# FFN-out's second Strassen half with accumulating loads on POOL, a shifted finish, and RG-LRU's input products placed later

## The chip, the cores and the metric

The kernel runs on one core of one Trainium2 chip. The metric is the device time of one execution in microseconds; the median of several executions counts. One more execution, made with the hardware profiler, gives the profile and the trace from which the rows below are.

## The reference

A hybrid encoder layer on 1024 + 512 positions of width 1024, float32. The parts that the change touches:

```python
xc = _centred_dwconv(xr, conv_w, conv_b)
rec = _rglru(xc, ..., False) + _rglru(xc, ..., True)
...
r = sigmoid(einsum(xb, wa) + ba)
i = sigmoid(einsum(xb, wx) + bx)
log_a = -RG_C * r * softplus(-lam)
a = exp(log_a)
u = sqrt(-expm1(2.0 * log_a)) * (i * xf)
_, h = associative_scan(comb, (a, u), reverse=reverse, axis=1)
...
fg, fu = split(h2 @ w_ffn_in, 2, axis=-1)
ff = (silu(fg) * fu) @ w_ffn_out
x = x + gt2[:, None] * ff
...
return _rmsnorm(x, final_g)
```

The hidden width of the FFN is 2816, in 22 column blocks of 128. Branch A (convolution, two RG-LRUs) stands early in the program, then come attention, the merge, FFN-in and, at the end, FFN-out.

## The kernel before

Every float32 product is three matmuls on high and low parts (hi·hi, hi·lo, lo·hi). The high part is a cast on ACT, the low part a subtraction on DVE, so each operand passes ACT and then DVE. Engines run their own instructions in the order of the program text; the text weaves helpers between matmuls by hand (`slots`, `bbuild`, `aprep`, the table `late`).

**RG-LRU** works on eight column blocks j of 128 channels, each a tile of 128 x 1536. While PE computes block j's input and its gate column, ACT and DVE finish the block before it. For each direction dd (0, 1) `decay(dd)` does on DVE L550 and L551 (from ACT's exponential and tanh) and L552, the input product i·xc; `roots(dd)` does on ACT L558 and L559 (square root; needs a table load); `scan(dd)` does on DVE L565 and the scans L570. `csplit` makes the high and low part xs of the next block (ACT L518, DVE L519), `gw_split` those of its gate weights (ACT L499, DVE L500). `gate(cc, dd)` multiplies xs by ghi and glo on PE (L532 to L534) into a bank of PSUM, and ACT empties it through a sigmoid into r and i (L535). `second` spreads these over six slots. Eleven buffers are passed around, so that the new i can take the place of one that the scan of the block before still reads.

**FFN-out** is one level of Strassen: seven products (PRODO, in the order 3, 1, 5, 2, 4, 6, 7), each of eleven K blocks and six pairs of row tiles. A step is one product for one pair: 33 matmuls, and there are 42 steps (n). The B operand of a product is a half of `w_ffn_out` or the sum or difference of two: products 3 and 4 subtract, 1, 6 and 7 add, 5 and 2 take one half alone. `bload` brings the two halves of a weight (256 KB each) by SP into one of two buffers, `bbuild` combines them (DVE L1274), casts (ACT L1275) and subtracts (DVE L1278). The A operands come by POOL (`aload`, L1306, 704 KB), are combined if need be (L1322), cast (L1323) and split (L1326). `take` adds a finished product to the accumulators `acc` (12 row tiles of 1024, in halves F1 and F2).

**The seam.** FFN-in's last products (PE L1446 to L1448 on tiles top, slot, woh, wol; emptied by ACT L1464 to L1478 and DVE L1468 to L1496; its weights combined at L1375 and split at L1359; results stored by SP, L1451, to ffd and ffx) run while `bbuild` makes the first eleven weights.

**The finish.** When the last product has been added to a half of `acc`, `squares` multiplies it by gt2 (DVE L1554), adds x1 (L1555; loaded by SP), and ACT squares and sums it (L1557). `norm1` and `norm2` make the row factors, `fin` scales both halves (DVE L1581) and stores them from POOL. The table `late` says at which step and K block. The last step's 512 columns are done in two parts of 256 (L1714 to L1717 for each) and closed by the last norm and two stores.

## Time and profile before

| | us |
|---|---|
| median of 3 executions | 2866.76 (2866.01 to 2868.51) |
| profiled execution | 2862.92 |
| its span | 2861.0 |
| PE busy | 2787.7 (97%) |
| DVE busy | 1925.6 (67%) |
| ACT busy | 1212.4 (42%) |
| POOL busy | 266.0 (9%) |

The span runs from the first to the last instruction of the profiled execution; 1.9 us of its time lie outside. Busy shares are means over all stages. A timeline row tells when an instruction started, how long it took and what its engine waited for ahead of it; a row of PE's waits tells what it waited for, us in total, how often, and the longest. A window row has the stretch, its length, busy time (and instructions) of PE, PE's weight loads, DVE, ACT and POOL, then the granted clock as a share of full speed, the DMA engines' share, and GB/s.

### The profile page before, as it was taken

How to read it: one execution, taken by the hardware profiler on the slowest of the kernel's cores; microseconds unless marked ns; L12 is line 12 of the kernel's file. 1: busy time of each engine (PE TensorE's matmuls, PEld its weight loads, DVE VectorE, ACT ScalarE, POOL GpSimd, SP SyncE). 2: the span in 40 equal slices, each digit the busy share in tenths (PEclk: the TensorE clock that was granted, in tenths of full speed). 3: DMA queues.
4: the chain of work that ended last, by engine and by line, in shares of the span. 5: the costliest groups of instructions: out<-in, count | busy, mean ns of one | idle time of the engine just before them, and what ended most of it. 6: DMA issues, size and time to landing. Idle time of an engine off the chain costs nothing. (4 is left out here: it accounts for less than half of the span.)

```text
span 2861.0 us, 38290 instructions
## 1 busy us (share of the span) xinstructions
PE 2787.7 (97%) x14165; PEld 2340.4 (82%) x14165; DVE 1925.6 (67%) x3615; ACT 1212.4 (42%) x2384; POOL 266.0 (9%) x365
## 2 busy tenths in 40 slices
PE   8999999999999999999999999999999999999997
PEld 4877777877777777777778877799999999977886
DVE  7487777555555555554367856599889888766787
ACT  6375766333333333224432015454444444344443
POOL 0000000000000000000153331101000000001002
PEclk9999999999999999999999999999999999999998
DMA  6211011201011011111367764567544444386685
GB/s 238 69 36 67 34 54 48 77 30 34 34 34 35 34 37 37 40 34 52 108 215 272 243 201 127 177 195 209 163 132 156 137 117 123 121 275 245 224 268 186
DMA packets 184395, 351.55 MB, mean 123 GB/s; under 512 B 20264, under 2 KB 99496, under 8 KB 183952
## 3 DMA queue, kind: packets, MB, share of 16 engines
q1 hardware_dynamic: 160016, 254.21, 28.0%
q0 software_dynamic: 24048, 94.63, 9.6%
q8 instruction: 111, 1.82, 0.3%
q14 instruction: 76, 0.62, 0.1%
q10 hardware_dynamic: 144, 0.26, 0.0%
HBM read 264.19 MB, written 84.85 MB: 122 GB/s over the span
## 5 line engine op out<-in xcount | busy, mean ns | idle before, releaser
L159 PE MATMUL mm<-hh,whi 128*128 128x512 f32 x1632 | 662.4, 406 | 2.8 <-DVE hh L292 2.3
L161 PE MATMUL mm<-hh,wlo 128*128 128x512 f32 x1632 | 641.3, 393 | 0.0
L160 PE MATMUL mm<-hl,whi 128*128 128x512 f32 x1632 | 639.7, 392 | 1.0 <-DVE hl L293 0.8
L159 PEld LDWEIGHTS mm<-hh,whi 128*128 128x128 f32 x1632 | 311.2, 191 | 71.3 <-issue 7.2
L161 PEld LDWEIGHTS mm<-hh,wlo 128*128 128x128 f32 x1632 | 307.5, 188 | 68.3
L160 PEld LDWEIGHTS mm<-hl,whi 128*128 128x128 f32 x1632 | 309.0, 189 | 63.5 <-DVE hl L293 4.4
L150 DVE TENSOR_TENSOR wlo<-wraw,whi 128x1024 fp32r<-128x1024 f32 x94 | 115.5, 1235 | 196.2 <-ACT whi L149 196.1
L747 ACT ACTIVATE sm<-sm,sg 128x192 f32<-128x192 f32 (+2 forms) x288 | 114.3, 397 | 303.4 <-DVE sg L742 303.0
L149 ACT CAST whi<-wraw 128x1024 fp32r<-128x1024 f32 x96 | 96.3, 1005 | 197.7 <-PE mm L160 124.4
L1375 DVE TENSOR_TENSOR sum<-wf 128x512 f32<-128x512 f32 x220 | 155.4, 707 | 1.5
L1377 ACT CAST woh<-sum 128x512 fp32r<-128x512 f32 x148 | 92.0, 622 | 151.4 <-DVE sum L1375 146.5
L742 DVE CUSTOM_DVE_ANT_0 sm<-sd,mk 128x192 f32<-128x192 f32 (+2 forms) x288 | 72.9, 291 | 117.0 <-PE sd L735 64.3
L668 DVE SCALAR_TENSOR_TENSOR t<-mm,rp 128x512 f32<-128x512 f32 x72 | 49.8, 692 | 150.2 <-PE mm L161 150.2
L1446 PE MATMUL mm<-top,woh 128*128 128x384 f32 x348 | 116.7, 335 | 3.3 <-DVE flat L1479 3.2
L1448 PE MATMUL mm<-top,woh 128*128 128x384 f32 x348 | 116.3, 334 | 0.0
L1447 PE MATMUL mm<-top,woh 128*128 128x384 f32 x348 | 116.2, 334 | 0.0
L1359 DVE TENSOR_TENSOR woh<-sum,woh 128x512 fp32r<-128x512 f32 x148 | 101.1, 683 | 0.6 <-ACT woh L1377 0.5
L857 DVE CUSTOM_DVE_ANT_0 jk<-ada 128x1024 bf16<-128x1024 f32 x64 | 80.5, 1271 | 23.6 <-DMA ada<-in_w_ada_dram 16.1
L1448 PE MATMUL sd<-top,woh 128*128 128x384 f32 x240 | 80.2, 334 | 0.0
L1446 PE MATMUL sd<-top,woh 128*128 128x384 f32 x240 | 80.2, 334 | 0.0
L1447 PE MATMUL sd<-top,woh 128*128 128x384 f32 x240 | 80.2, 334 | 0.0
L161 PE MATMUL mm<-rh,wlo 128*128 128x512 f32 x192 | 75.2, 392 | 3.8 <-DVE wlo L150 3.8
(452 smaller groups left out, 6386.6 us busy)
## 6 DMA issues: line engine op xcount, KB each, us to landing
wf<-in_w_fi_dram SPq DMA_DIRECT2D x88, 512.0 KB, 4.0
wraw<-in_w_in_dram SPq DMA_DIRECT2D x68, 512.0 KB, 3.5
wo<-in_w_fo_dram SPq DMA_DIRECT2D x132, 256.0 KB, 4.2
ffd<-flat SPq DMA_DIRECT2D x88, 192.0 KB, 4.0
ada<-in_w_ada_dram SPq DMA_DIRECT2D x32, 512.0 KB, 4.3
ffx<-flat SPq DMA_DIRECT2D x66, 192.0 KB, 2.3
wol<-ffd POOLq DMA_DIRECT2D x18, 704.0 KB, 4.9
gated<-gs POOLq DMA_DIRECT2D x48, 256.0 KB, 3.1
```

The costliest lines, as they stand in the source:

```text
L149: s.copy(out=hi, in_=t)
L150: eng.tensor_tensor(out=lo, in0=t, in1=hi.bitcast(F32), op=ALU.subtract)
L159: pe.matmul(ps, lhsT=hi(k), rhs=xh(k), start=a, stop=False)
L160: pe.matmul(ps, lhsT=hi(k), rhs=xl(k), start=False, stop=False)
L161: pe.matmul(ps, lhsT=lo(k), rhs=xh(k), start=False, stop=z)
L747: s.activation(out=sm[:, c], in_=sm[:, c], func=AF.Exp, scale=-1.0, bias=sg[:, u, x:x + 1], accum_out=sg[:, u, x + 1:x + 2])
L1359: v.tensor_tensor(out=r[:, CH:], in0=t, in1=f32(r[:, :CH]), op=ALU.subtract)
L1375: v.tensor_tensor(out=t, in0=wraws[p, a], in1=wraws[p, b], op=op)
L1377: s.copy(out=r[:, :CH], in_=t)
L1446: pe.matmul(ps, lhsT=hi, rhs=bh[:, k], start=k == 0 and not more, stop=False, skip_group_check=more)
L1447: pe.matmul(ps, lhsT=hi, rhs=bl[:, k], start=False, stop=False, skip_group_check=more)
L1448: pe.matmul(ps, lhsT=lo, rhs=bh[:, k], start=False, stop=k == 3, skip_group_check=more)
```

## The change

**RG-LRU.** `decay` loses the input product; it becomes `inputs(dd)`, and `second` has the two decays in slots one and two, ahead of `csplit` and `gw_split`, and the two input products in slot four.

On DVE, from a block's last convolution to its second scan, before (a, r and i are the two directions' tiles, xs and glo the next block's operands):

```order
 L550 SCALAR_TENSOR_TENSOR a_1427<-a_1427,r_1275 128x1536
 L551 SCALAR_TENSOR_TENSOR r_1275<-a_1427 128x1536
 L552 TENSOR_TENSOR i_1276<-i_1276,xc 128x1536
 L519 TENSOR_TENSOR xs_1459<-xc,xs_1458 128x1536
 L500 TENSOR_TENSOR glo_762<-graw,ghi_761 64x4x64 x2
 L550 SCALAR_TENSOR_TENSOR a_1430<-a_1430,r_1349 128x1536
 L551 SCALAR_TENSOR_TENSOR r_1349<-a_1430 128x1536
 L552 TENSOR_TENSOR i_1350<-i_1350,xc 128x1536
 L565 TENSOR_TENSOR i_1276<-i_1276,r_1275 128x1536
```

and now:

```order
 L550 SCALAR_TENSOR_TENSOR a_1427<-a_1427,r_1275 128x1536
 L551 SCALAR_TENSOR_TENSOR r_1275<-a_1427 128x1536
 L550 SCALAR_TENSOR_TENSOR a_1430<-a_1430,r_1349 128x1536
 L551 SCALAR_TENSOR_TENSOR r_1349<-a_1430 128x1536
 L519 TENSOR_TENSOR xs_1473<-xc,xs_1472 128x1536
 L500 TENSOR_TENSOR glo_762<-graw,ghi_761 64x4x64 x2
 L557 TENSOR_TENSOR i_1276<-i_1276,xc 128x1536
 L557 TENSOR_TENSOR i_1350<-i_1350,xc 128x1536
 L570 TENSOR_TENSOR i_1276<-i_1276,r_1275 128x1536
```

The second L551 moved ahead of three others, L519 and L500 moved back by one instruction's time, and the first product with r (L565, now L570) stands where it stood.

**The weights of FFN-out.** Their loads go from SP to POOL, the A operands' from POOL to SP. For the products that add, the second half is loaded with an accumulating transfer on top of the first (`accum_op`), so the DVE addition goes and a weight needs half a buffer: four weights are in flight instead of two. A base load is issued when the low part of the weight that held its place is done, the accumulating load one weight later. The first load stands one column earlier, low parts are put off to the next column or slot (`lows`, `flush`), and the first A operands are prepared over two columns.

POOL's queue at the change from the subtracting product to the adding one, now (L1296 loads a first half, L1298 a subtracted one, L1303 accumulates; 19295 and 19296 are the two buffers, each with two halves):

```order
 L1296 DMA wo_19295<-in_w_fo_dram 128x512
 L1298 DMA wo_19295<-in_w_fo_dram 128x512
 L1296 DMA wo_19296<-in_w_fo_dram 128x512
 L1296 DMA wo_19295<-in_w_fo_dram 128x512 x2
 L1296 DMA wo_19296<-in_w_fo_dram 128x512
 L1303 DMA wo_19296<-in_w_fo_dram 128x512
 L1296 DMA wo_19296<-in_w_fo_dram 128x512
 L1303 DMA wo_19295<-in_w_fo_dram 128x512 x2
 L1303 DMA wo_19296<-in_w_fo_dram 128x512
 L1296 DMA wo_19295<-in_w_fo_dram 128x512
```

The same weights on SP before, where a pair is one weight:

```order
 L1263 DMA wo_19510<-in_w_fo_dram 128x512 x2
 L1263 DMA wo_19529<-in_w_fo_dram 128x512 x2
 L1263 DMA wo_19569<-in_w_fo_dram 128x512 x2
 L1263 DMA wo_19588<-in_w_fo_dram 128x512 x2
 L1263 DMA wo_19608<-in_w_fo_dram 128x512 x2
```

Weight 10's two halves are followed by the bases of 11 to 14 with 11's accumulating load behind the third of them, and 12's accumulating load stands behind the base of 15.

**The finish.** `gated2` multiplies on DVE and lets POOL accumulate x1 from DRAM onto `acc`; ACT's squares come a step later (K block 6), or at K block 8 in the last product. `late` has the norms and `fin`s one to three steps earlier, and `fin` stores from SP. In the last step one half of row tile 7 and one of tile 8 still get x1 by a DVE addition.

DVE behind the last step's first matmuls, before (acc_19643, 19647 and 19648 are row tiles 2, 6 and 7, scaled at the end):

```order
 L1540 TENSOR_TENSOR acc_19648<-acc_19648,mm 128x512
 L1554 TENSOR_TENSOR acc_19648<-acc_19648,gt_19654 128x512
 L1555 TENSOR_TENSOR acc_19648<-acc_19648,slot 128x512
 L1565 TENSOR_TENSOR st<-st 128x1
 L1566 TENSOR_SCALAR st<-st 128x1
 L1581 SCALAR_TENSOR_TENSOR acc_19643<-acc_19643,st,fgb 128x512 x2
 L1581 SCALAR_TENSOR_TENSOR acc_19647<-acc_19647,st,fgb 128x512 x2
```

and now (19638 is tile 7, 19637 tile 6):

```order
 L1584 TENSOR_TENSOR acc_19638<-acc_19638,mm 128x512
 L1750 TENSOR_TENSOR acc_19638<-acc_19638,gt_19644 128x512
 L1751 TENSOR_TENSOR acc_19638<-acc_19638,slot 128x512
 L1609 RECIPROCAL st<-st 128x1
 L1610 TENSOR_TENSOR st<-st 128x1
 L1611 TENSOR_TENSOR st<-st 128x1
 L1612 TENSOR_SCALAR st<-st 128x1
 L1613 TENSOR_TENSOR st<-st 128x1
 L1618 SCALAR_TENSOR_TENSOR acc_19637<-acc_19637,st,fgb 128x512 x2
```

Tile 2 is scaled ahead of tile 7's addition now, and tile 6's factor is made there.

```diff
@@ -546,9 +546,14 @@
             def decay(dd):
 
                 def f():
-                    r, i, a0 = R[f"r{dd}"], R[f"i{dd}"], R[f"a{dd}"]
+                    r, a0 = R[f"r{dd}"], R[f"a{dd}"]
                     v.scalar_tensor_tensor(out=a0, in0=a0, scalar=1.0, in1=r, op0=ALU.add, op1=ALU.mult)
                     v.scalar_tensor_tensor(out=r, in0=a0, scalar=2.0, in1=a0, op0=ALU.subtract, op1=ALU.mult)
+                return f
+            def inputs(dd):
+                def f():
+                    i = R[f"i{dd}"]
                     v.tensor_tensor(out=i, in0=i, in1=R["xc"], op=ALU.mult)
                 return f
 
@@ -602,7 +608,8 @@
             C, CS = ([c["C"]], [c["CS"]]) if c else ([], [])
             gs = [lambda: gw_split(j)] if c else []
             if p:
-                slots([p["X"]] + C + [p["E"][0]], CS + gs + [p["Q"][0]], [p["E"][1]], [p["Q"][1]], [p["S"][0]], [p["GE"]])
+                slots([p["X"]] + C + [p["E"][0]], [p["E"][1]], CS + gs + [p["Q"][0]],
+                      [p["I"][0], p["Q"][1], p["I"][1]], [p["S"][0]], [p["GE"]])
             else:
                 slots(C, gs, CS, [], [], [])
 
@@ -1245,38 +1252,72 @@
     NSTEP = len(PRODO) * len(PAIRS)
     bslot = [slot[i][:, D * e:D * (e + 1)] for i in (5, 2, 0, 1) for e in range(4)]
     upper = [f32(slot[i][:, 3 * D:]) for i in (3, 4)]
-    braw = {}
+    brawt = []
     araw = [f32(slot[i][:, :2 * AH]) for i in (4, 3)]
     acmb = []
+    lows = []
+    def flush(fs=None):
+        for f in list(lows if fs is None else fs):
+            lows.remove(f)
+            f()
     a0 = {}
-    nbl, nbb = [0], [0]
-    def bload(upto):
-        while nbl[0] < min(upto, len(PRODO) * KH):
-            q, k = divmod(nbl[0], KH)
...
+    NB = len(PRODO) * KH
+    def bkind(n):
+        return PRODO[n // KH][2][2] == ALU.subtract
+    def bplace(n):
+        return {2 * (n % 2), 2 * (n % 2) + 1} if bkind(n) else {n % 4}
+    def braw(n):
+        o = 2 * (n % 2) if bkind(n) else n % 4
+        return brawt[o // 2][:, o % 2 * CH:]
+    def bpart(n, e):
+        q, k = divmod(n, KH)
+        nm = PRODO[q][2][e]
+        i, j = int(nm[0]) - 1, int(nm[1]) - 1
+        return w_fo[KH * i + k, :, j * CH:(j + 1) * CH]
+    def bload():
+        if not brawt:
+            brawt.extend(wts.tile([P, D], F32, tag="raw", name="wo2") for _ in range(2))
+        top = nbl[0]
+        while nbl[0] < NB and not any(bplace(nbl[0]) & bplace(m) for m in range(nlow[0], nbl[0])):
+            n = nbl[0]
             nbl[0] += 1
-            for e, nm in enumerate(PRODO[q][2][:2]):
-                if nm:
-                    i, j = int(nm[0]) - 1, int(nm[1]) - 1
-                    sp.dma_start(out=t[:, e * CH:(e + 1) * CH], in_=w_fo[KH * i + k, :, j * CH:(j + 1) * CH])
+            g_.dma_start(out=braw(n)[:, :CH], in_=bpart(n, 0))
+            if bkind(n):
+                g_.dma_start(out=braw(n)[:, CH:], in_=bpart(n, 1))
+        while nba[0] < max(top, nbb[0]):
+            n = nba[0]
+            nba[0] += 1
+            if PRODO[n // KH][2][2] == ALU.add:
+                g_.dma_start(out=braw(n)[:, :CH], in_=bpart(n, 1), accum_op=ALU.add)
 
     def bbuild(upto, later=None):
 
-        while nbb[0] < min(upto, len(PRODO) * KH):
+        while nbb[0] < min(upto, NB):
             n = nbb[0]
-            bload(n + 1)
             nbb[0] += 1
-            t, r = braw.pop(n), bslot[n % 20]
-            op = PRODO[n // KH][2][2]
-            if op is not None:
-                v.tensor_tensor(out=t[:, :CH], in0=t[:, :CH], in1=t[:, CH:], op=op)
+            if n >= nba[0]:
+                bload()
+            t, r = braw(n), bslot[n % 20]
+            if bkind(n):
+                v.tensor_tensor(out=t[:, :CH], in0=t[:, :CH], in1=t[:, CH:], op=ALU.subtract)
             s.copy(out=r[:, :CH], in_=t[:, :CH])
 
-            def low(n=n, t=t, r=r):
+            def low(t=t, r=r):
                 v.tensor_tensor(out=r[:, CH:], in0=t[:, :CH], in1=f32(r[:, :CH]), op=ALU.subtract)
-                bload(n + 3)
+                nlow[0] += 1
+                bload()
             if later is None:
                 low()
             else:
@@ -1303,7 +1344,7 @@
                 sp.dma_start(out=a0["raw"][e][:, :w], in_=asrc("11", 0)[:, o:o + w])
             return
         for e, nm in enumerate(PRODO[q][1]):
-            g_.dma_start(out=araw[n % 2][:, e * AH:(e + 1) * AH], in_=asrc(nm, i))
+            sp.dma_start(out=araw[n % 2][:, e * AH:(e + 1) * AH], in_=asrc(nm, i))
 
     def aprep(n, i, later=None):
 
@@ -1508,17 +1549,20 @@
                 pass1(0)
             if 0 <= m - M1 - 5 <= 10 and (m - M1 - 5) % 2 == 0:
                 pass1((m - M1 - 5) // 2 + 1)
-            if p == 2 * NFF - 3 and c == 6:
-                bload(2)
+            if p == 2 * NFF - 3 and c == 5:
+                bload()
+            if p >= 2 * NFF - 2:
+                flush()
             if p == 2 * NFF - 2:
-                bbuild((1, 2, 3, 4, 5, 6, 6)[c])
+                bbuild((1, 2, 3, 4, 5, 6, 6)[c], lows)
             if p == 2 * NFF - 1:
                 if c == 0:
                     aload(0)
-                bbuild((7, 8, 8, 9, 10, 11, 11)[c])
-                if c == 2:
-                    for i in range(3):
-                        aprep(0, i)
+                bbuild((7, 8, 8, 9, 10, 11, 11)[c], lows)
+                if c in (2, 3):
+                    for i in ((0, 1), (2,))[c - 2]:
+                        aprep(0, i, lows)
+                if c == 3:
                     aload(1)
 
     tops.close()
@@ -1539,22 +1583,15 @@
             a = acc[t][:, f]
             v.tensor_tensor(out=a, in0=a, in1=ps, op=op)
 
-        nx = [0]
-        def x1load(t, f):
-            e, m = divmod(nx[0] % 4, 2)
-            nx[0] += 1
-            a = upper[e][:, m * CH:(m + 1) * CH]
-            sp.dma_start(out=a, in_=x1d[t * P:(t + 1) * P, f])
-            return a
-        def squares(t, f, xo, ps):
+        def gated2(t, f):
 
             a = acc[t][:, f]
             v.tensor_tensor(out=a, in0=a, in1=gt2[t // 8][:, f], op=ALU.mult)
-            v.tensor_tensor(out=a, in0=a, in1=xo, op=ALU.add)
+            g_.dma_start(out=a, in_=x1d[t * P:(t + 1) * P, f], accum_op=ALU.add)
+        def squares(t, f, ps):
             e = f.start // CH
-            s.activation(out=ps, in_=a, func=AF.Square, accum_out=st[:, 2 * t + e:2 * t + e + 1])
+            s.activation(out=ps, in_=acc[t][:, f], func=AF.Square, accum_out=st[:, 2 * t + e:2 * t + e + 1])
 
         rs = st[:, 48:60]
 
@@ -1579,7 +1616,7 @@
             a, r = acc[t], rs[:, t:t + 1]
             for f in (F2, F1):
                 v.scalar_tensor_tensor(out=a[:, f], in0=a[:, f], scalar=r, in1=fgb[:, f], op0=ALU.mult, op1=ALU.mult)
-                g_.dma_start(out=dest(t)[:, f], in_=a[:, f])
+                sp.dma_start(out=dest(t)[:, f], in_=a[:, f])
 
         def take(n, ps):
 
@@ -1621,26 +1658,23 @@
         M7 = 6 * len(PAIRS)
         late = {}
         for n, k, f in (
-            (M7 - 2, 6, lambda: norm1(3, 3)), (M7 - 2, 9, lambda: norm2(3, 3)),
-            (M7 - 1, 9, lambda: fin(3)), (M7, 9, lambda: fin(4)), (M7 + 1, 9, lambda: fin(5)),
...
-            (M7 + 4, 6, lambda: fin(0)), (M7 + 4, 10, lambda: (fin(1), norm1(2, 1), norm1(6, 1))),
...
+            (M7 - 2, 10, lambda: norm1(3, 3)), (M7 - 1, 3, lambda: norm2(3, 3)), (M7 - 1, 9, lambda: fin(3)),
+            (M7, 6, lambda: fin(4)), (M7, 9, lambda: fin(5)),
...
+            (M7 + 3, 9, lambda: fin(1)),
...
         ):
             late[n, k] = f
 
...
         ps = None
+        todo = []
+        upper = [a[:, :CH] for a in upper]
         tl = PAIRS[-1]
         aload(2)
+        flush()
         for i in range(3):
             aprep(1, i, lows)
             if i:
@@ -1649,7 +1683,7 @@
         for n in range(NSTEP - 1):
             q, i = divmod(n, len(PAIRS))
             before, ps = ps, (sdb if n % 2 else mmb)()
-            done = xo = None
+            done = None
             for k in range(KH):
                 mms(ps, n, k)
                 if k == 0 and n:
@@ -1659,8 +1693,9 @@
                         done = take(n - 1, before)
                     if q == 3 or done and done[1] is F2 and done[0] in PAIRS:
                         done = (PAIRS[i], F2) if q == 3 else None
-                    if done:
-                        xo = x1load(*done)
+                    if done and q == 6:
+                        gated2(*done)
+                        todo.append(done)
                     flush()
                     aload(n + 3)
                 elif k in (2, 5):
@@ -1670,6 +1705,8 @@
                     flush(had)
                 elif k in (3, 6):
                     flush()
+                    if k == 6 and q < 6 and todo:
+                        squares(*todo.pop(0), before)
                 elif k == 4:
                     aprep(n + 2, 0, lows)
                 elif k == 7:
@@ -1681,12 +1718,18 @@
                             sp.dma_start(out=gt2[e], in_=src.rearrange("p a d -> p (a d)"))
                 elif k == 9:
                     flush()
-                    if done:
-                        squares(*done, xo, before)
+                    if done and q < 6:
+                        gated2(*done)
+                        todo.append(done)
+                if k == 8 and q == 6:
+                    while todo:
+                        squares(*todo.pop(0), before)
                 if (n, k) in late:
                     late[n, k]()
             if n == NSTEP - 3:
-                xl = x1load(tl, F1)
+                xl, xn = upper
+                for a, t in ((xl, tl), (xn, tl - 1)):
+                    sp.dma_start(out=a, in_=x1d[t * P:(t + 1) * P, F1])
             if n == NSTEP - 2:
 
                 a = acc[tl]
@@ -1702,13 +1745,15 @@
             for k in range(KH):
                 mms(pl, n, k, cols)
                 if e == 0 and k == 1:
-                    late[n, 0]()
-                    done = take(n - 1, ps)
-                    squares(*done, x1load(*done), ps)
+                    take(n - 1, ps)
+                    c = acc[tl - 1][:, F1]
+                    v.tensor_tensor(out=c, in0=c, in1=gt2[0][:, F1], op=ALU.mult)
+                    v.tensor_tensor(out=c, in0=c, in1=xn, op=ALU.add)
+                    squares(tl - 1, F1, ps)
+                    norm2(6, 1)
+                    fin(6)
                     norm1(7, 1)
-                if e == 0 and k == 6:
-                    fin(2)
-                    fin(6)
+                if e == 0 and k == 10:
                     norm2(7, 1)
                     fin(7)
             v.tensor_tensor(out=b[:, cols], in0=pl, in1=gt2[1][:, cols], op=ALU.mult)
```

## Rows read from the trace of the kernel before

**Rows 1.** The page, busy time and share of the span by engine.

```profile
PE 2787.7 (97%) x14165; PEld 2340.4 (82%) x14165; DVE 1925.6 (67%) x3615; ACT 1212.4 (42%) x2384; POOL 266.0 (9%) x365
```

**Rows 2.** PE's waits, 100 to 500 us; windows around three stalls.

```profile
PE sd L532 <- ACT r L535: 17.3, 5, 3.5
...
165.00:185.00 20.00, 16.53 (x72) 13.15 (x71) 15.98 (x11) 13.03 (x16) 0.54 (x1) 1.00 0.20 73
210.00:230.00 20.00, 16.53 (x65) 13.00 (x64) 16.02 (x12) 13.08 (x16) 0.55 (x1) 0.91 0.18 66
315.00:335.00 20.00, 16.54 (x60) 12.92 (x59) 15.27 (x11) 12.22 (x16) 0.54 (x1) 0.83 0.19 66
```

**Rows 3.** The timeline of the second block: start, duration, engine, line, [idle before].

```profile
155.54 1.75 DVE L552 TENSOR_TENSOR i<-i,xc 128x1536 f32<-128x1536 f32 x1
...
161.57 1.76 DVE L551 SCALAR_TENSOR_TENSOR r<-a 128x1536 f32<-128x1536 f32 x1
...
166.70 3.41 DVE L570 TENSOR_TENSOR_SCAN r<-a,i 128x1024 f32<-128x1024 f32 x2
...
159.85 0.57 ACT L473 COPY gg<-mm 128x512 f32<-128x512 f32 x1
163.36 1.49 ACT L558 ACTIVATE a<-a 128x1536 f32<-128x1536 f32 x1 [2.95 <-DVE r L551]
...
171.74 0.69 ACT L535 ACTIVATE r<-sd,gb 128x512 f32<-128x512 f32 x1
...
160.98 0.39 PE L534 MATMUL sd<-xs,glo 128*128 128x512 f32 x1
...
172.48 0.50 PE L532 MATMUL sd<-xs,ghi 128*128 128x512 f32 x1 [3.47 <-ACT r L535]
```

**Rows 4.** PE's waits, 2480 us to the end (columns as in rows 2).

```profile
PE mm L1446 <- ACT flat L1464: 3.5, 1, 3.5
PE mm L1616 <- ACT woh L1275: 1.7, 1, 1.7
PE sd L1446 <- DVE flat L1468: 1.6, 1, 1.6
PE sd L1618 <- DVE a1lo L1326: 1.4, 1, 1.4
PE mm L1616 <- ACT wol L1275: 1.1, 1, 1.1
```

**Rows 5.** Windows of the seam and of the end (columns as in rows 2).

```profile
2480.00:2500.00 20.00, 18.28 (x104) 17.64 (x103) 13.51 (x24) 6.89 (x12) 0.58 (x1) 1.00 0.56 171
2500.00:2520.00 20.00, 16.49 (x75) 15.10 (x74) 14.34 (x26) 6.31 (x12) 0.55 (x1) 0.83 0.78 256
2520.00:2540.00 20.00, 16.64 (x61) 12.47 (x60) 14.02 (x24) 8.80 (x17) 1.06 (x2) 0.83 0.81 249
...
2740.00:2840.00 100.00, 100.00 (x470) 83.98 (x469) 84.52 (x154) 41.06 (x87) 14.22 (x27) 1.00 0.73 238
```

**Rows 6.** Timeline of SP's queue and of DVE at the first weight.

```profile
2482.92 17.27 SPq L1263 DMA_DIRECT2D wo<-in_w_fo_dram  x11
...
2487.24 0.69 DVE L1274 TENSOR_TENSOR wo<-wo 128x512 f32<-128x512 f32 x1 [3.66 <-DMA wo<-in_w_fo_dram]
```

**Rows 7.** DMA issues: KB each, median us to landing; the whole span, then 2470 to 2530.

```profile
wo<-in_w_fo_dram SPq DMA_DIRECT2D x132, 256.0 KB, 4.2
...
slot<-ffd POOLq DMA_DIRECT2D x17, 704.0 KB, 5.8
...
wo<-in_w_fo_dram SPq DMA_DIRECT2D x26, 256.0 KB, 3.5
```

**Rows 8.** The timeline's end on PE and DVE (columns as in rows 3).

```profile
2840.76 0.28 PE L1618 MATMUL mm<-a0hi,a1lo 128*128 128x256 f32 x1
...
2850.67 1.42 DVE L1581 SCALAR_TENSOR_TENSOR acc<-acc,st,fgb 128x512 f32<-128x512 f32 x2
...
2853.53 0.42 DVE L1714 TENSOR_TENSOR b<-mm,gt 128x256 f32<-128x256 f32 x1
```

More of the change, by code (lines that the diff above doesn't have):

```diff
@@ L581, in fin @@
                 g_.dma_start(out=rnnd[j], in_=e0)
-            return dict(R=R, C=conv, CS=csplit, X=exps, E=[decay(0), decay(1)], Q=[roots(0), roots(1)], GE=gelu, S=[scan(0), scan(1)], F=fin,
+            return dict(R=R, C=conv, CS=csplit, X=exps, E=[decay(0), decay(1)],
+                           I=[inputs(0), inputs(1)], Q=[roots(0), roots(1)], GE=gelu, S=[scan(0), scan(1)], F=fin,
                            G=[[gate(cc, dd) for cc in range(NCH)] for dd in range(2)])
@@ L1247, in encoder_kernel @@
     upper = [f32(slot[i][:, 3 * D:]) for i in (3, 4)]
-    braw = {}
+    brawt = []
     araw = [f32(slot[i][:, :2 * AH]) for i in (4, 3)]
     acmb = []
-    a0 = {}
-    nbl, nbb = [0], [0]
-    def bload(upto):
-        while nbl[0] < min(upto, len(PRODO) * KH):
-            q, k = divmod(nbl[0], KH)
-            t = braw[nbl[0]] = wts.tile([P, D], F32, tag="raw", name="wo2")
-            nbl[0] += 1
-            for e, nm in enumerate(PRODO[q][2][:2]):
-                if nm:
-                    i, j = int(nm[0]) - 1, int(nm[1]) - 1
-                    sp.dma_start(out=t[:, e * CH:(e + 1) * CH], in_=w_fo[KH * i + k, :, j * CH:(j + 1) * CH])
+    lows = []
@@ new lines, in flush @@
+    def flush(fs=None):
+        for f in list(lows if fs is None else fs):
+            lows.remove(f)
+            f()
+    a0 = {}
+    nbl, nba, nbb, nlow = [0], [0], [0], [0]
+    NB = len(PRODO) * KH
[11 more added lines that the diff above has]
+        return w_fo[KH * i + k, :, j * CH:(j + 1) * CH]
@@ L1623, in encoder_kernel @@
         for n, k, f in (
-            (M7 - 2, 6, lambda: norm1(3, 3)), (M7 - 2, 9, lambda: norm2(3, 3)),
-            (M7 - 1, 9, lambda: fin(3)), (M7, 9, lambda: fin(4)), (M7 + 1, 9, lambda: fin(5)),
-            (M7 + 1, 6, lambda: norm1(9, 3)), (M7 + 2, 1, lambda: norm2(9, 3)),
-            (M7 + 2, 9, lambda: fin(9)), (M7 + 3, 9, lambda: fin(10)), (M7 + 4, 1, lambda: fin(11)),
-            (M7 + 3, 6, lambda: norm1(0, 2)), (M7 + 4, 3, lambda: norm2(0, 2)),
-            (M7 + 4, 6, lambda: fin(0)), (M7 + 4, 10, lambda: (fin(1), norm1(2, 1), norm1(6, 1))),
-            (M7 + 5, 0, lambda: (norm2(2, 1), norm2(6, 1))),
+            (M7 - 2, 10, lambda: norm1(3, 3)), (M7 - 1, 3, lambda: norm2(3, 3)), (M7 - 1, 9, lambda: fin(3)),
+            (M7, 6, lambda: fin(4)), (M7, 9, lambda: fin(5)),
+            (M7, 10, lambda: norm1(9, 3)), (M7 + 1, 3, lambda: norm2(9, 3)), (M7 + 1, 6, lambda: fin(9)),
+            (M7 + 2, 6, lambda: fin(10)), (M7 + 2, 9, lambda: fin(11)),
+            (M7 + 2, 10, lambda: norm1(0, 2)), (M7 + 3, 3, lambda: norm2(0, 2)), (M7 + 3, 6, lambda: fin(0)),
+            (M7 + 3, 9, lambda: fin(1)),
+            (M7 + 3, 10, lambda: norm1(2, 1)), (M7 + 4, 3, lambda: norm2(2, 1)), (M7 + 4, 6, lambda: fin(2)),
+            (M7 + 4, 10, lambda: norm1(6, 1)),
         ):
             late[n, k] = f
-        lows = []
-        def flush(fs=None):
-            for f in list(lows if fs is None else fs):
-                lows.remove(f)
-                f()
         ps = None
+        todo = []
+        upper = [a[:, :CH] for a in upper]
         tl = PAIRS[-1]
         aload(2)
+        flush()
         for i in range(3):
```

## The prediction

> **What bounds the kernel now.** I first read the busy shares [rows 1]. PE is busy 2787.7 us of 2861.0, so only about 73 us are open to a change that leaves PE's work alone, as this one does; DVE at 67% and ACT at 42% can cost time only where PE waits for them, or behind PE's last matmul. Next I asked what PE waited for in the stretches that the diff touches. There are three places.
>
> RG-LRU, 100 to 500 us: one kind of stall, five times, 17.3 us together, each 3.5 us: PE's gate product waits for ACT to empty a bank into r [rows 2]. The granted clock falls behind four of the five: in windows of 20 us around them it reads 1.00, 0.91 and 0.83 at the first three [rows 2], and at the other two as at the second. It steps between 2.4 GHz and 1.2 GHz, so a window's shortfall is time lost: 0.09 + 0.17 + 0.09 + 0.09 = 0.44 of 20 us, 8.8 us. Each window holds one stall.
>
> The seam, 2480 to 2540 us, where the last FFN-in products and the first FFN-out steps share the engines: waits of 3.5, 1.7, 1.6 and 1.4 us, and later one of 1.1 [rows 4]; the clock reads 1.00 over the 20 us to 2500, which hold the 1.6, and 0.83 over each of the next two 20 us, which hold the 3.5 and the pair of 1.7 and 1.4 [rows 5]: 2 x 3.4 us gone besides the waits. From there to the last matmul PE is 100% busy in a window of 100 us [rows 5]: nothing can be won between but by fewer waits, and the 40 steps from 2538 to 2841 take 7.5 us each.
>
> The end: PE's last matmul starts at 2840.76, the span ends at 2861.0: 20 us of tail, in which DVE works off a backlog. DVE is still scaling finished rows from 2850.67 to 2852.0, and the last half's own chain starts only behind that, its second part at 2853.53 [rows 8]. From that start to the end are 7.5 us.
>
> **The change part by part.**
>
> *RG-LRU.* On DVE the order for one chunk was L550, L551, L552 (0), L519, L500, L550, L551, L552 (1). ACT's L558 (1) waited for L551 (1), which starts at 161.57 behind L552 at 155.54, L519 and L500; it ran at 163.36 after 2.95 us idle, with its last other work, L473, at 159.85 [rows 3]. After, the two pairs L550/L551 stand together: the second L551 ends at 155.54 + 2 x 1.75 = 159.0, so L558 follows L473 at 160.42, 2.94 us earlier, and everything behind it on ACT moves with it: r from 171.74 to 168.8, its bank free at 169.5. PE arrived at 172.48 - 3.47 = 169.01 [rows 3]. Two things become late instead. L519 and L500 now stand behind both pairs, from 159.0 to 161.6 (1.67 and 0.86 us), and PE's first product that reads glo, L534, was there at 160.98 [rows 3]: a new wait of 0.6 us, which brings PE to r's bank at 169.6, when it is free. And i overwrites what scan 0 reads; the scan, at 166.70 for 3.41 us, doesn't move, because DVE has the same instructions ahead of it; i ends at 170.1 + 0.7 = 170.8, and PE, three matmuls of 0.23 us behind 169.6, waits 0.5 us. So 1.1 to 1.2 us stays of 3.47: five times 2.3 = **-11.6**. The input products moved back, 2 x 1.75 us, are hidden: DVE has them done at 165, as before.
>
> The clock: the trace has no pair of 0.6 and 0.5 us, 9 us apart, here. Bounds: none of the 8.8 us comes back, or all. The nearest row is the single gap of 1.6 us before 2500 [rows 4], behind which the clock stays at 2.4 GHz [rows 5], against 3.5 us with a fall four times in five. Both new gaps are shorter, so I take all of it: **-8.8** (0 to -8.8).
>
> *Seam.* The weights' loads were issued on SP behind the stores of differences: the first at 2482.92, and its subtraction ran at 2487.24, after 3.66 us idle [rows 6]. On POOL nothing stands ahead of it but the wait for the buffer's last reader, so the load is there when DVE comes to the subtraction, at 2487.24 - 3.66 = 2483.6: 3.7 us earlier. But the cycle behind it is unchanged for these subtract kinds: two buffers, a load that takes about 4.2 us to land (3.5 in the seam alone) [rows 7], three DVE and ACT pieces of 0.6 to 0.7: about 3.7 us a weight, and a low part that is put off to the next slot gives some of the lead back. Walked by hand through the new order, weight 7's subtraction now waits for its load on DVE with the combination that empties PE's bank queued behind it: a new PE wait of about 4.6 us near 2505 in place of the 3.5; weight 10 is cast some 3.7 us earlier; step 0 ends 1.9 and step 1 some 2.6 to 4 us earlier. Against that stands the start of the accumulating loads: the add for weight 12 stands on POOL behind the base load of weight 15, which waits for the low part of weight 11. Its cast, late, stands on ACT ahead of step 2's A operand: 1 to 3 us. With landings from 3.5 to 4.8 us the whole runs from -7 to +3; **-2**. Later one step waits 1.1 us for a late weight [rows 4]; bases issued four weights ahead may cure that: **-1** (0 to -3, with what small waits of DVE's pieces it drags behind it).
>
> *Accumulating loads in steady state.* 33 weights (three products of 11) lose their DVE addition of 0.69 us, 23 us in all, and 22 additions of x1 go, 0.69 each. PE has no wait there [rows 4, 5], so this is worth nothing before the end. No row shows an accumulating load; the plain ones of the same size take 4.2 us, POOL's larger ones up to 5.8 [rows 7], and the price of landing late is bounded in the rivals.
>
> *Tail.* In the last steps DVE loses an addition a step, and the scalings of rows stand two or three steps earlier. After the end of step 40, at 2841 - 8.1 = 2832.9, DVE still has: one pair of scalings 1.4, small ones 0.4, acc 8's three operations 2.05, acc 7's three 2.05, normalising 1.35, a pair 1.4, normalising 1.35, a pair 1.35: 11.4 us, of which the first 3.9 can run before. So DVE is free 7.5 to 11.4 us after 2832.9, at 2840.4 to 2844.3, instead of 2852.0. The first part's chain takes 1.5 us, then from the second part's start 7.5 to the end: 2849.4 to 2853.3 on the old clock, against 2861.0. All hidden it would be 2848.6. **-10** (-7.7 to -12.4).
>
> The Trainium skill speaks against moving loads to POOL: "SBUF — State Buffer", section "A bandwidth-pool intuition that's wrong (but worth ruling out)", tells of a load from GpSimd's queue that took 3100 ns instead of 620 beside a DVE copy, because its descriptors couldn't be written meanwhile. By that, an estimate, each seam load would land 2.5 us later and the time would come to about 2847; POOL's loads of 704 KB, which land within 5.8 us beside a DVE that is 85% busy [rows 5, 7], mostly with two-input operations, don't bear it out.
>
> Sum: -11.6 - 8.8 - 2 - 1 - 10 = -33.4, from the profiled 2862.9 to 2829.5. The median of the runs before, 2866.8, lies 3.8 us above the profiled execution; with that 2833.
>
> **Rivals.**
>
> 1. *The clock falls still* behind the two new waits. Twice within a few microseconds, by 1.7 and 1.4 us, PE stood in the seam, and there it did fall [rows 4, 5]. Then the 8.8 us stay: 2842.
>
> 2. *The seam is cured.* If loads land in 3.5 us or less and the staggered preparation empties DVE's queue, the seam's waits, 3.5 + 1.7 + 1.6 + 1.4, and the clock's 6.8 go, 15.0 in place of the 2 that I count: 2833 - 13 = 2820. Against it: the cycle of two buffers has not changed.
>
> 3. *Loads from POOL land later in the seam.* If the 256 KB land like the slowest of POOL's large loads, 5.8 us [rows 7], instead of 3.5, each of two buffers comes round 2.3 us later, so a weight costs 1.15 us more: 11 weights, 12.7 us, 2846; more if the clock stays down longer. For it: DMA is busy for 0.78 and 0.81 of these windows and 0.73 later [rows 5], and nothing was loaded so from POOL before. Against: bytes explain POOL's long landings at least as well.
>
> 4. *Slower: accumulating loads outlast their lead.* A step of 7.5 us with 11 weights in six steps is 4.1 us a weight, four half-buffers 16.3 us. In them go: issue and landing of the base 4.7, issue 0.5, the add's landing X, cast 0.6, low part with its delay 2.1. So from X = 8.4 on each weight costs (X - 8.4)/4, 33 times, because a late add blocks ACT's queue and with it the A operands. The 39.5 us that turn the forecast into a loss above 2872 need X = 13.2, three times the plain load; then 2873 or more. For it: both the base and an addition now cross the same engines at 0.73 share [rows 5].
>
> 5. *It doesn't do what it says in RG-LRU*: r waits for something other than ACT's order, and the five gaps stay with their falls: 2833 + 20 = 2853.
>
> **How the numbers follow.** Forecast 0.50 (its own bounds 2823 to 2841), rival 1 0.15, rival 2 0.15, rival 3 0.08, rival 4 0.06, rival 5 0.06. A measurement here tells about 0.2%, 5.7 us, from no change. All but rival 4 are faster by more, and of rivals 3 and 5 the far ends come near: faster 0.92, same 0.03, slower 0.05. The range 2816 to 2850 holds the forecast, rivals 1 and 2 with some of their ends left out, and half of rival 3; rivals 4 and 5 lie outside.
>
> **What would show it.** RG-LRU right: no wait for r or short ones, waits for glo (L500) of about 0.6 and for i of about 0.5, five of each, and clock windows of 1.00. Wrong: the r wait still over 3 us. Seam right: first weight subtraction near 2483.6 less 20, one PE wait of 4 to 5 us for an emptied bank, and a new one in step 2. Accumulating loads: a landing under 8 us, and no PE wait for a cast between step 3 and the end. Tail: last matmul to span's end 8.5 to 12.5 us, with DVE's last pair of scalings before or just behind PE's end. The forecast is wrong as a whole if PE's stretch of 100% [rows 5] shows waits in the three products with additions.

## The result and the profile after

The changed kernel takes 2890.0 us (median; 2885.3 to 2895.7) against 2867.6 before: slower by 0.8%, ratio 1.0079 with a 95% interval of 1.0060 to 1.0098. The forecast was 2833, in a range up to 2850. Its profiled execution has a span of 2888.7 us, 27.7 more than before. From the page, the lines that answer to [rows 1]; the landings that answer to [rows 7] stand further down:

```profile
span 2888.7 us, 38252 instructions
PE 2798.2 (97%) x14165; PEld 2340.3 (81%) x14165; DVE 1887.9 (65%) x3560; ACT 1209.7 (42%) x2384; POOL 328.0 (11%) x444
```

DVE lost its work, 37.7 us. PE's busy time rose by 10.5 with the same matmuls; the mean granted clock of the whole execution hardly changed (0.990 before, 0.989 after). RG-LRU came out as hoped. PE's waits from 100 to 500 us, and windows around the first two places of [rows 2] (same columns):

```profile
PE sd L532 <- ACT i L535: 2.6, 5, 0.5
PE sd L534 <- DVE glo L500: 1.4, 5, 0.3
...
165.00:185.00 20.00, 19.46 (x85) 15.45 (x84) 16.31 (x12) 11.39 (x16) 0.54 (x1) 1.00 0.21 73
205.00:225.00 20.00, 19.49 (x85) 15.46 (x84) 18.39 (x13) 12.61 (x16) 0.55 (x1) 1.00 0.11 37
```

The five waits for r are gone, 0.5 us for i and 0.3 us for glo stand in their place, and the clock no longer falls (1.00 from 100 to 500 us, 0.98 before). PE's waits from 2400 us to the end, which answer to [rows 4], tell where the time went:

```profile
PE mm L1653 <- ACT a0hi L1364: 23.8, 9, 4.2
PE sd L1487 <- DVE flat L1509: 5.0, 1, 5.0
PE mm L1654 <- DVE woh L1318: 2.7, 1, 2.7
PE sd L1653 <- ACT a1hi L1364: 2.2, 1, 2.2
```

Nine waits for the cast of an A operand, up to 4.2 us, in a stretch that had none before: two around step 2, the others from step 26 on. The stretch that was 100% busy in [rows 5] (2740 to 2840) now reads, with 20 us ahead of it:

```profile
2720.00:2760.00 40.00, 32.65 (x132) 25.65 (x132) 18.73 (x31) 12.79 (x27) 14.13 (x19) 0.96 0.92 210
2760.00:2800.00 40.00, 34.56 (x132) 26.44 (x132) 18.04 (x30) 13.74 (x31) 14.03 (x19) 0.91 0.81 190
2800.00:2840.00 40.00, 34.39 (x144) 26.49 (x144) 21.28 (x40) 13.13 (x28) 7.47 (x9) 1.00 0.69 165
```

Every step of FFN-out begins with a matmul that changes the bank, so the timeline gives each step's length; 7.48 us is one without a wait. The difference of the two spans is then a sum:

| stretch | before, us | after, us | difference |
|---|---|---|---|
| start to step 0 | 2516.29 | 2504.60 | -11.7 |
| steps 0, 1, 2 | 10.13, 11.53, 7.48 | 12.73, 11.86, 13.23 | +8.7 |
| steps 3 to 25 | 175.3 | 173.6 | -1.8 |
| steps 26 to 40 | 112.2 | 145.9 | +33.7 |
| step 41 to the end | 28.0 | 26.8 | -1.2 |

Of the 33.7 us, 21.9 are PE's waits in these steps. The granted clock is 0.95 over their 146 us, which takes about another 7 (an estimate: 0.05 x 146); the rest stays unassigned.

Why ACT is late is in its own waits, 2500 us to the end (columns as in [rows 4]):

```profile
ACT sd L1594 <- DMA acc<-x1d: 49.2, 9, 7.8
ACT mm L1594 <- DMA acc<-x1d: 35.9, 8, 7.0
...
ACT wol L1315 <- DMA wo<-in_w_fo_dram: 16.0, 5, 7.6
ACT woh L1315 <- DMA wo<-in_w_fo_dram: 13.7, 2, 13.2
```

ACT stood 85 us before its squares (L1594) for x1's accumulating transfer, and some 40 before the weights' casts. Its queue runs in order, and A's casts (L1364) stand behind both. The transfers themselves, 2530 to 2870 us (KB each, median us to landing):

```profile
wo<-in_w_fo_dram POOLq DMA_DIRECT2D x105, 256.0 KB, 4.7
...
acc<-x1d POOLq DMA_DIRECT2D x22, 256.0 KB, 6.2
```

The first row mixes plain loads with accumulating ones. Taken by line, the plain first halves land in 3.9 us (median), the 33 accumulating ones in 3.7 to 9.6, 6.5 in the median.

Two mechanisms can be read at single steps. Around step 26 the first weights of the second adding product are made. From ACT's and POOL's timelines:

```profile
2714.65 0.62 ACT L1315 CAST wol<-wo 128x512 fp32r<-128x512 f32 x1 [7.59 <-DMA wo<-in_w_fo_dram]
2715.18 0.61 ACT L1364 CAST a0hi<-slot 128x512 fp32r<-128x512 f32 x1
2721.35 0.62 ACT L1315 CAST a0hi<-wo 128x512 fp32r<-128x512 f32 x1 [5.56 <-DMA wo<-in_w_fo_dram]
...
2707.46 0.93 POOL L1303 DMA_DIRECT2D wo<-in_w_fo_dram  x1
2708.01 1.27 POOL L1590 DMA_DIRECT2D acc<-x1d  x1
2716.29 0.57 POOL L1296 DMA_DIRECT2D wo<-in_w_fo_dram  x1 [7.00 <-DVE wol L1318]
2716.84 2.65 POOL L1303 DMA_DIRECT2D wo<-in_w_fo_dram  x3
```

The first weight's addition is issued at 2707.46 and lands at 2714.65. The second's stands on POOL behind a base load that waits for the first weight's low part, so it is issued only at 2716.84 and lands 4.5 us later: two landings, one after the other, and A's next casts wait behind both. Steps 27 and 28 run like this (POOL's timeline, then ACT's):

```profile
2732.50 0.85 POOL L1303 DMA_DIRECT2D wo<-in_w_fo_dram  x1 [4.09 <-DMA wo<-in_w_fo_dram]
2733.05 1.17 POOL L1590 DMA_DIRECT2D acc<-x1d  x1
...
2740.05 0.60 ACT L1594 ACTIVATE sd<-acc 128x512 f32<-128x512 f32 x1 [5.94 <-DMA acc<-x1d]
```

Here DVE had its product for x1 ready at 2728.50. POOL stood 4.09 us for a base load to land, since an addition may be issued only on top of a landed base; x1's transfer waited behind it, landed seven microseconds after its issue, and ACT's squares waited 5.94 us.

### The profile page after: what moved, and what is told of

It is laid out like the page before. It is cut to its first block, busy times and chain, and to the rows that moved or that the text cites. A ratio compares the mean times of both kernels' runs of the same rounds, so it can differ in the third digit from the quotient of the medians.

```text
span 2888.7 us, 38252 instructions
## 1 busy us (share of the span) xinstructions
PE 2798.2 (97%) x14165; PEld 2340.3 (81%) x14165; DVE 1887.9 (65%) x3560; ACT 1209.7 (42%) x2384; POOL 328.0 (11%) x444
## 3 DMA queue, kind: packets, MB, share of 16 engines
q0 software_dynamic: 30496, 91.03, 10.9%
## 5 line engine op out<-in xcount | busy, mean ns | idle before, releaser
L1296 POOL DMA_DIRECT2D wo<-in_w_fo_dram x77 | 47.2, 614 | 613.9 <-DVE woh L1400 441.9
L864 DVE CUSTOM_DVE_ANT_0 jk<-ada 128x1024 bf16<-128x1024 f32 x64 | 80.3, 1267 | 25.8 <-DMA ada<-in_w_ada_dram 17.3
L806 POOL DMA_DIRECT2D od<-of x24 | 13.1, 547 | 635.3 <-ACT qb L727 354.4
L1489 PE MATMUL sd<-top,woh 128*128 128x384 f32 x240 | 80.2, 334 | 0.0
```

The costliest lines, as they stand in the source:

```text
L1489: pe.matmul(ps, lhsT=lo, rhs=bh[:, k], start=False, stop=k == 3, skip_group_check=more)
```

## Experiments

Two theories after the result: (1) x1's accumulating transfers, on which ACT's squares wait in order, cost steps 26 to 41; (2) the weights' accumulating loads, late for their casts, do. Each ratio is to the kernel before, timed beside it.

**RG-LRU alone.** The kernel before with this only:

```diff
-                slots([p["X"]] + C + [p["E"][0]], CS + gs + [p["Q"][0]], [p["E"][1]], [p["Q"][1]], [p["S"][0]], [p["GE"]])
+                slots([p["X"]] + C + [p["E"][0]], [p["E"][1]], CS + gs + [p["Q"][0]],
+                      [p["I"][0], p["Q"][1], p["I"][1]], [p["S"][0]], [p["GE"]])
```

> The kernel before with nothing but RG-LRU's new order. The trace of the changed kernel shows its later stages 18.7 us earlier until about 1500 us, so both theories expect 2867.6 - 18.7 = 2849 us (2846 to 2852), with no falls of the clock at RG-LRU. If the gain were lost again in the stages between (4 to 5 us seem to be, from 1525 to 1709 us), 2853.

Measured: 2850.1 us, ratio 0.9929 (0.9914 to 0.9944). As expected; this part alone is worth 17 to 20 us, and the rest of the change costs 40.

**x1 on DVE again.** The changed kernel with

```diff
-            g_.dma_start(out=a, in_=x1d[t * P:(t + 1) * P, f], accum_op=ALU.add)
+            v.tensor_tensor(out=a, in0=a, in1=xo, op=ALU.add)
```

and x1 loaded by SP (`xo`), squares right behind.

> The changed kernel, but x1 is loaded by SP into a buffer and added on DVE again, with the squares right behind; the weights' accumulating loads stay. Theory 1 (ACT's squares wait in order for x1's accumulating transfer, and the A operands' casts stand behind them): nearly all of the 33.7 us that steps 25 to 41 lose, and some 5 us of the tail, go: 2890 - 35 = 2855 (2850 to 2862). Theory 2 (the weights' accumulating loads come late and block ACT's casts): at most 8 us go: 2882 or more.

Measured: 2856.3 us, ratio 0.9950 (0.9935 to 0.9964). That is what theory 1 gives. Steps 27 to 40 all take 7.5 us; steps 2 and 26 still take 13.1 and 12.8. From PE's last matmul to the end there are 14.6 us, against 19.0 in the changed kernel.

**Weights' sums on DVE again.**

```diff
-        return PRODO[n // KH][2][2] == ALU.subtract
+        return PRODO[n // KH][2][2] is not None
...
-            if PRODO[n // KH][2][2] == ALU.add:
-                g_.dma_start(out=braw(n)[:, :CH], in_=bpart(n, 1), accum_op=ALU.add)
```

> The changed kernel, but the weights' sums are made on DVE again, both halves loaded plainly from POOL into two buffers; x1's accumulating transfers stay. Theory 1: POOL no longer waits for a base load ahead of x1's transfer, so 5 to 12 us go, but ACT still waits for each transfer: 2878 to 2885. Theory 2: the 33.7 us of steps 25 to 41 go, 2850 to 2860.

Measured: 2861.2 us, ratio 0.9966 (0.9955 to 0.9978): far below what theory 1 gives and a little above theory 2. Steps 2 and 26 take 7.5 us, while seven of the steps 28 to 38 still lose 0.5 to 3 each. Neither theory holds by itself: either half taken back heals most.

**Addition ahead of the next base.** The loop that issues additions moved before the loop that issues bases:

```diff
         top = nbl[0]
+        while nba[0] < max(top, nbb[0]):
+            ...
         while nbl[0] < NB and not any(bplace(nbl[0]) & bplace(m) for m in range(nlow[0], nbl[0])):
```

> The changed kernel with one thing turned round on POOL: a weight's accumulating load is issued ahead of the next base load, so it no longer stands behind a base that waits for a low part. If the starts of the adding products are what that order costs (step 26 took 13.9 us in place of 7.5, step 2 13.2): 6 to 12 us less, 2878 to 2884. If POOL's waits for landing bases only move: within 3 us of 2890.

Measured: 2923.0 us, ratio 1.0185 (1.0168 to 1.0203): a miss on the other side. POOL's waits ahead of an addition (columns as in [rows 4]), 2500 us to the end, here:

```profile
POOL wo L1297 <- DMA wo<-in_w_fo_dram: 137.8, 30, 7.6
```

and in the changed kernel:

```profile
POOL wo L1303 <- DMA wo<-in_w_fo_dram: 49.9, 14, 5.4
```

POOL now stands for nearly every base's landing before it may issue the next one, and all behind it in its queue is later. Though unforeseen, it points at the queue: with both kinds of transfer in it, more standing of POOL, more loss.

**Squares later.** The changed kernel; before the last product `squares` moved from K block 6 to 9.

> The changed kernel, but in the products before the last ACT's squares wait for x1's transfer three K blocks (2 us) later in the step; every transfer stays as it was. If ACT's place in order behind x1's landing is what blocks the A operands (theory 1): most of the 18.5 us that steps 28 to 35 lose go, 2890 - 14 = 2876 (2870 to 2882); steps 26, 36 and 38 keep their losses (6.5, 3.9 and 4.8 us). If ACT is blocked by the weights' casts (theory 2): within 3 us of 2890.

Measured: 2873.8 us, ratio 1.0018 (1.0007 to 1.0030), 16 us less than the changed kernel. In the trace steps 28 to 35 lose 8.3 us in place of 18.5, and step 26 takes 10.5 in place of 13.9, which was not expected. Another 3.4 us lie ahead of step 0, where both kernels are the same. No transfer was changed, so ACT's place in order behind x1's landing is shown as a cause.

**Both on DVE.** Both edits above together.

> The changed kernel with both kinds of accumulating load taken back: the weights' sums and x1 on DVE, weights still loaded by POOL, the finish and the seam as changed. If the two accumulating loads are the whole loss, steps 2 and 26 take 7.5 us as with the weights' sums on DVE, steps 27 to 41 take 7.5 us as with x1 on DVE, and the tail is 14.5 us: 2844 (2841 to 2849). If DVE, with 56 more operations, becomes late: 2850 or more.

Measured: 2846.6 us, ratio 0.9928 (0.9908 to 0.9949). PE is busy all of both windows here, though DVE has its additions back:

```profile
2740.00:2780.00 40.00, 40.00 (x178) 33.15 (x177) 32.26 (x54) 19.03 (x39) 9.88 (x19) 1.00 0.73 257
2780.00:2820.00 40.00, 40.00 (x191) 33.66 (x190) 36.95 (x79) 12.75 (x31) 0.00 (x0) 1.00 0.66 212
```

So of the two kinds, in medians over 2846.6: weights alone +9.7, x1 alone +14.7, both +43.5; in the traces, counted from step 0, +9.4, +14.3 and +40.9. The 17 to 19 us above the sum had to come from how they meet. The waits show it (columns as in [rows 4], 2500 us to the end; POOL's with the weights alone, then ACT's with x1 alone, where L1590 are the squares):

```profile
POOL wo L1303 <- DMA wo<-in_w_fo_dram: 49.6, 21, 5.7
...
ACT sd L1590 <- DMA acc<-x1d: 30.9, 12, 6.6
ACT mm L1590 <- DMA acc<-x1d: 23.8, 7, 6.3
```

With the weights alone POOL stands for landing bases as long as in the changed kernel (49.9 us), and steps 27 to 40 lose nothing by it: no transfer of x1 stands behind. For x1's transfers ACT stands 55 us with x1 alone and 85 with both. The DMA engines' load by itself is not enough: with the weights' kind alone the same window runs at a share of 1.00 and PE is never late (the row is that kernel's):

```profile
2740.00:2780.00 40.00, 40.00 (x178) 33.11 (x177) 29.59 (x49) 18.06 (x39) 13.96 (x20) 1.00 1.00 277
```

**Addition two weights behind its base.** The changed kernel; `btop` keeps the earlier tops:

```diff
-        while nba[0] < max(top, nbb[0]):
+        while nba[0] < max(btop[-2], nbb[0]):
```

> The changed kernel, but a weight's accumulating load is issued two weights behind its base load, not one, so that the base has landed when POOL comes to it; all transfers and ACT's order stay. The two kinds of accumulating load cost 9.7 us (weights alone) and 14.7 us (x1 alone) but 43.5 us together. If the 19 us above the sum are POOL standing still for a landing base with x1's transfer behind it in its queue: POOL's 49.9 us of such waits fall below 15, and 2890 - 16 = 2874 (2868 to 2880). If they are the DMA engines' load: within 5 us of 2890. If the add, now later, misses its own cast: 2895 or more.

Measured: 2881.6 us, ratio 1.0042 (1.0024 to 1.0059). POOL's waits for a landing base, 49.9 us in the changed kernel, are gone: the list of its waits has no such row, only those for DVE and x1's products, of which the longest two are

```profile
POOL acc L1591 <- DVE acc L1590: 70.7, 19, 11.3
POOL wo L1297 <- DVE woh L1319: 70.7, 22, 10.2
```

Steps 27 to 32, which lost 13.4 us, lose nothing any more; ACT's waits for x1 fell from 85 to 60 us. x1's transfers, as many as before, landed 5.2 us after their issue in the median; it was 6.2 in the changed kernel and 5.1 with x1 alone. All that fits POOL standing for a landing with x1's transfer behind it as the place where the two meet. But the total fell by 8 only, half of what was expected: steps 5, 6, 25 and 26 lose 14.6 us where the changed kernel loses 6.5, while adding products' weights are made. The additions now come too late for their casts: ACT's waits for weights rose from 43 us (five rows) to 79. So how much of the 17 to 19 us POOL's standing accounts for stays open. (The profiled execution, 2887.6, is the slowest of its six.)

**Low parts at once in the seam**, on the kernel with both on DVE: `bbuild(..., lows)` back to `bbuild(...)` in the seam's two calls.

> As the kernel with both kinds on DVE, but the weights' low parts in the seam are made at once, not a column later. If the put-off low part delays the next load (two buffers), the 4.9 us wait for an emptied bank shrinks and step 0 begins or ends 2 to 4 us earlier: 2841. If it only moves the waits: within 1.5 us of the kernel with both on DVE.

Measured: 2843.0 us, ratio 0.9911 (0.9891 to 0.9930). The wait for an emptied bank fell from 5.1 to 1.6 us, and step 0 began 2.5 and ended 4.3 us earlier, as expected of the put-off low parts. But step 1 took 11.9 in place of 8.7, so step 3 began only 1.1 us earlier. The intervals of the two kernels overlap.

**RG-LRU and the finish.** The kernel before with RG-LRU's order, the new `late` table, stores from SP and the new last step; x1 on DVE.

> The kernel before with RG-LRU's new order and the new finish (norms and scalings earlier, stores from SP, last step's order), x1 added on DVE, weights from SP and A operands from POOL as before. The tail from the last matmul was 19.4 us with RG-LRU alone and 14.5 with x1 on DVE in the changed kernel: 2850 - 5 = 2845 (2842 to 2848). If the new finish owes its gain to fewer DVE additions of weights, 2850.

Measured: 2846.2 us, ratio 0.9922 (0.9901 to 0.9943). From PE's last matmul to the end its trace has 18.6 us, against 19.6 with RG-LRU alone and 20.2 before: the finish is worth about one microsecond there. The total lies in the range expected of the finish, but the 5 us behind the last matmul did not come, so the finish is not what put it there. DVE's timeline tells why (step 41 began at 2818.16, PE's last matmul at 2825.96):

```profile
2818.62 0.68 DVE L1547 TENSOR_TENSOR acc<-acc,sd 128x512 f32<-128x512 f32 x1
...
2824.55 0.69 DVE L1562 TENSOR_TENSOR acc<-acc,slot 128x512 f32<-128x512 f32 x1 [1.72 <-DMA slot<-x1d]
2826.03 0.16 DVE L1572 TENSOR_TENSOR st<-st 128x1 f32<-128x1 f32 x1 [0.79 <-ACT sd L1564]
...
2828.22 0.68 DVE L1547 TENSOR_TENSOR acc<-acc,mm 128x512 f32<-128x512 f32 x1
```

The first L1547 takes in step 39, whose product was done at 2810.68: DVE is a whole step behind, and waits besides.

**Stores back on POOL**, on the kernel with low parts at once.

> The kernel with both kinds on DVE and low parts at once in the seam (2843), with the finished rows' stores back on POOL. On SP, x1's loads stand behind stores that wait for DVE, and DVE waits 1.7 to 2.3 us for x1 behind the last steps. If that wait is on the path to the end: 2841. If DVE's backlog hides it: 2843 within 1.5 us.

Measured: 2841.9 us, ratio 0.9912 (0.9895 to 0.9930): not to be told from 2843.0.

**x1 added by a POOL operation**, on the same kernel; squares a step later as in the change.

> The same kernel (2843), with x1 added by a POOL operation instead of DVE's, and ACT's squares later in the step as in the changed kernel. POOL's two-input operations of this size took 1.4 to 1.8 us elsewhere, less than a transfer's 4 to 8. If DVE's backlog sets the end: the last six steps lose 6 x 0.69 = 4 us of DVE, 2839 (2836 to 2842). If the squares' waiting for POOL blocks ACT as x1's transfers did: 2847 or more.

Measured: 2840.9 us, ratio 0.9907 (0.9889 to 0.9925). Steps 4 to 40 but one take 7.5 us, and POOL's addition took 1.3 to 1.4 us. From PE's last matmul to the end there are 14.7 us against 18.4 in the kernel with low parts at once, the 4 us that were expected if DVE's backlog sets the end; step 3, at 11.4 in place of 8.3, took most of them back in this trace. Inside the interval of the others, but the best median, 0.9% under the kernel before and 1.7% under the changed one. That x1's addition may leave DVE, if nothing waits long for it, fits all of the above.

## Why the prediction was wrong, point by point

- **RG-LRU, -11.6 and -8.8: right.** 13.3 us of waits went (17.3 to 4.0), and the clock's falls with them; alone it measured -19.9 in medians. The two new waits were those named, L500's 0.3 in place of 0.6. Rivals 1 and 5 fall. In the changed kernel's trace 5 of the 18.7 us of lead are lost again before 2480 us, most of them between 1600 and 1710; 3.7 with RG-LRU alone, 0.3 with both on DVE. Why stays open.
- **Seam, -2: wrong by about 13.** The wait for the emptied bank came as forecast (5.0 us for 4.6). The late additions came too, but they cost 9 us in place of 1 to 3: steps 1 and 2 took 25.1 us, against 16.2 with the sums on DVE. Two were late, and I had priced one. ACT's timeline:

```profile
2528.00 0.62 ACT L1315 CAST woh<-wo 128x512 fp32r<-128x512 f32 x1 [13.16 <-DMA wo<-in_w_fo_dram]
...
2534.59 0.62 ACT L1315 CAST wol<-wo 128x512 fp32r<-128x512 f32 x1 [5.45 <-DMA wo<-in_w_fo_dram]
```

The first, weight 11's, stands on POOL behind the base of 14 (the fourth base, not the third), was issued at 2518.40 and landed 9.6 us later; PE's first matmul of step 2 waited 3.3 us for the A operand cast behind it. The second, 12's, cost PE another 1.9, and the clock read 0.85 over steps 0 to 2. Against RG-LRU alone, step 3 began at 2542.4 and not at 2531.6: +10.9. With the sums on DVE it begins at 2530.3, so loading by POOL and the staggered seam cost nothing; POOL's loads landed in 3.6 us there (median, 2470 to 2530 us), and rival 3 falls. The same start at step 26 (6.5 us) was in the order I had read, and I did not count it a second time: that is the first step of the working that failed.
- **Later steps, -1: right in number, in part by luck.** Steps 11, 12 and 24 gained 1.8. But the wait for a late weight, at step 12, was 0.6 us here and 1.1 again with the squares later, which is the same kernel up to there, so the bases issued early did not cure it; RG-LRU alone, with the old loads, gained 1.2 in the same steps. Only step 24's 0.8 goes in every kernel with the new loads.
- **Accumulating loads in steady state, "worth nothing before the end": wrong, and the main error.** I priced a late weight (rival 4) by its landing and left out what shares its queues. An addition needs its base landed; POOL waits for that in order; x1's transfer stands behind; ACT's squares wait for x1 in order; A's casts stand behind the squares. Accumulating landings were 6.5 us for the weights (2 of 33 above rival 4's point of 8.4) and 6.2 for x1, in the median, and still PE lost 33.7 us in steps 26 to 40. Rival 4 had the right engines (ACT blocked, A late) and the wrong threshold; its tile, the weight, by itself cost 9 us, around steps 2 and 26 alone, and the rest came with x1's transfers. The prediction's own sign of being wrong as a whole, waits of PE in the products with additions, is what came.
- **Tail, -10: wrong.** 1.2 measured. The step that failed is "of which the first 3.9 can run before" the end of step 40: DVE was a whole step behind by then. It took step 40's product at 2872.57, 10.7 us after it was done, as late as before the change (10.9). Half of the forecast did come in the two kernels where x1's transfers were gone and DVE had one of the two additions less (x1 on DVE, x1 added by POOL): 14.6 and 14.7 us behind the last matmul, with that product taken 6 us late. In the changed kernel DVE also stood 3.2 us for squares that waited 5.85 us for x1's last transfer:

```profile
2870.38 0.16 DVE L1602 TENSOR_TENSOR st<-st 128x1 f32<-128x1 f32 x1 [3.17 <-ACT sd L1594]
...
2869.62 0.60 ACT L1594 ACTIVATE sd<-acc 128x512 f32<-128x512 f32 x1 [5.85 <-DMA acc<-x1d]
```

The range failed because every bound was a term's own: none was for two terms that meet in one queue, the 17 to 19 us that only both together cost. The rule that I weighed from the Trainium skill ("SBUF — State Buffer", section "A bandwidth-pool intuition that's wrong (but worth ruling out)") tells of a load from GpSimd's queue held up beside a DVE copy. Nothing of the kind shows here: with both kinds on DVE, POOL's plain loads land in 3.5 us (median, 2530 to 2840 us). DVE runs almost only two-input operations there, so the page's own case was not tried. The 5.8 us that the prediction set against it is a median; the slowest of those loads took 9.6. That additions must go through POOL's queue at all is what "DMA: Bandwidth & Descriptors", section "SWDGE vs HWDGE vs iDMA", of the Trainium skill states (accumulating only from GpSimd); no run here tried another engine.

## What to carry to other kernels

A wait that is harmless by its length is not harmless in an in-order queue: before moving work onto a transfer, list what stands behind the instruction that issues it and behind the one that waits for it, down to the operand that PE reads. Two changes that each pass this test may fail it together when they share an issuing queue, so time them apart and together. Taking operations off an engine that isn't the bound (DVE lost 37.7 us here) pays nothing where PE is always busy, and in a tail only as far as that engine's backlog shrinks by it (5 us in two kernels here, about one in the changed kernel).

## What the hardware showed

An accumulating transfer of 256 KB from POOL took 0.86 (x1) to 0.89 us (weights) of POOL's time to issue, in the median (0.54 to 0.56 for a plain one), and 3.9 to 8.7 us to land for x1 (6.2 in the median), 3.7 to 9.6 for the weights (6.5); plain ones land in 3.5 in the median with both kinds on DVE. DMA engines at a share of 1.00 over 40 us did not slow PE in the kernel with x1 on DVE. Two waits of 0.3 and 0.5 us, some 9 us apart, left the clock at 2.4 GHz, where one of 3.5 us had dropped it to 1.2 GHz four times in five.
